# Weighted one-hot rows in a routing-weight build: split over VectorE, GpSimd and ScalarE

## The chip, the cores and the metric

The kernel runs on one core of one Trainium2 chip. The metric is device microseconds for one execution of the whole program. In the text PE is TensorE, DVE is VectorE, ACT is ScalarE, POOL is GpSimd and SP is SyncE, which here only issues DMAs.

## The reference, cut to what matters

The reference is one transformer layer over 512 tokens of width 2048: adaptive norm, a hybrid mixer (attention beside a gated recurrence), and then a PEER expert layer, which is where the change lies. For each token and each of 8 heads PEER picks 16 of 16,384 experts:

```python
v1, i1 = lax.top_k(s1, 16)            # 128 first keys
v2, i2 = lax.top_k(s2, 16)            # 128 second keys
vs, ic = lax.top_k(v1[..., :, None] + v2[..., None, :], 16)
e = i1[ic // 16] * 128 + i2[ic % 16]
w = jax.nn.softmax(vs, axis=-1)
...
act = jax.nn.gelu(jnp.einsum('thkd,td->thk', u[e], hx)) * wx
y   = jnp.einsum('thk,thkd->td', act, vt[e])
```

So a token has 128 picks (8 heads by 16), each with a first key, a second key and a weight. There are 16,384 experts, 128 by 128.

## The kernel before

Tokens 128 to 511 (three groups of 128) go through the experts densely. `ublock(b)` multiplies 128 experts' rows of u with the tokens: two half blocks, each a 512 KB load (`raw`), a rounded copy on ScalarE (`shi`, L91), the remainder on VectorE (`slo`, L92, `src - hi`) and 24 matmuls (L685). `shi` and `slo` have three buffers each, so the split can run at most a few half blocks ahead of TensorE. There are 128 such blocks. Their results are written to DRAM tables `tab1` and `tab2` (L691, L692).

Beside them the routing weights are built as a dense matrix, token by token, in six half sets of 64 tokens (the loop at L872; `hf` counts them). For each token a one-hot matrix of its 128 picks by first key (`o1`, four tokens in one VectorE operation, L880) is multiplied by a matrix of its picks by second key that carries the weight (`o2`, one operation per token, L885): row k of `o2` is the pick's weight at the column of its second key and zero elsewhere. TensorE multiplies the two (L886, two passes each for float32), four tokens share a PSUM bank, and ScalarE copies the bank into `ws` (L887). I call four tokens a group; there are 16 groups in a half set, 96 in all, 384 `o2` in all. `o2` has six buffers, so row matrices can be made a group and a half ahead of TensorE. After a half set `ws` is written to DRAM (L892) and VectorE takes its maximum in four operations (`F`, L893). After half sets 3 and 5 (counted from 0), `make_list` makes lists of the experts in use, scattered by GpSimd DMAs (L859).

Tokens 0 to 127 go another way, as side work: 128 gathers of rows of u (issued by GpSimd, L761, into four `gr` buffers), each followed by a dot product on VectorE (L775), then 128 gathers of rows of v, each followed by a multiply-add on VectorE (L773).

When all blocks are done, `vrun` gathers rows of v by the lists and multiplies them with the tables (L946), for two list sets in turn; what is left of the side work runs beside the first. The last part adds the residual and normalizes; its `xr` tiles hold pieces of the residual.

The order on each engine is not the source's: a scheduler places every instruction on its engine by a modelled timeline when the program is built. Each engine then works through its own queue strictly in that order and waits at its head.

Of the kernel before, what the change touches and what calls it, by code (L numbers as in the profile page):

```python
# [9 lines left out]
F32 = mybir.dt.float32  # L10
# [4 lines left out]
AF = mybir.ActivationFunctionType  # L15
OP = mybir.AluOpType
# [10 lines left out]
ND = 3  # L27
# [29 lines left out]
def program(ctx: ExitStack, tc: tile.TileContext, a):  # L57
    nc = tc.nc
    V, A, PE, G = nc.vector, nc.scalar, nc.tensor, nc.gpsimd

    def pool(stack, name, bufs=1, **kw):
        return stack.enter_context(tc.tile_pool(name=name, bufs=bufs, reuse_waits="tile", **kw))
# [20 lines left out]
    iota = const.tile([128, 128], F32, name="iota")  # L83
# [79 lines left out]
    def bank():  # L163
        return ps.tile([128, 512], F32, name="ps", tag="ps")

    def pbank():
        return ps.tile([128, 512], F32, name="pj", tag="pj", bufs=2)

    for q in range(4):
        p = pbank()  # L170
# [7 lines left out]
    with tc.tile_pool(name="pro", bufs=1, reuse_waits="tile") as pro:  # L178
# [7 lines left out]
        for t in range(NT):  # L186
# [10 lines left out]
            for k4 in range(4):  # L197
                p = pbank()
# [27 lines left out]
    def wt(dt=F32):  # L226
        return wk.tile([128, 512], dt, name="w" if dt == F32 else "wr", tag="w")
# [33 lines left out]
    p = pbank()  # L261
# [9 lines left out]
    p = bank()  # L271
# [31 lines left out]
    scale = 128 ** -0.5  # L303
# [213 lines left out]
    for q in range(4):  # L517
# [18 lines left out]
        for t in range(NT):  # L536
            for h in held:
                out_mm(t, *h)
            xr = wt()
# [17 lines left out]
    with tc.tile_pool(name="wk2", bufs=12, reuse_waits="tile") as wk2:  # L557
        for q in range(4):
            pr = bank()
            for k4 in range(4):  # L560
                k = q * 4 + k4
                p = bank()
# [78 lines left out]
    for h in range(H):  # L641
# [6 lines left out]
        for half in range(2):  # L648
            p = pbank()
# [10 lines left out]
            p = bank()  # L660
# [34 lines left out]
    otp = pool(dn, "otp", side="right")  # L695
    gq = pool(dn, "gq", 2, side="right")
    oT = []
# [7 lines left out]
    def ublocks(upto):  # L705
        while blk[0] < upto:
            ublock(blk[0])
            blk[0] += 1

    for t in range(ND):  # L710
        se, wv = decode(tp, tts[t])
        p = bank()
        o = otp.tile([128, 3, 128], F32, name="oT", bufs=ND)
        for i, src in enumerate((se[:, 0], se[:, 1], wv)):
            PE.transpose(p[:, i * 128:i * 128 + 128], src.rearrange("p h k -> p (h k)"), ident)
        A.copy(o, p[:, :384].rearrange("p (i t) -> p i t", i=3))
        oT.append(o)
        ublocks(t + 1)
    tk.close()
# [150 lines left out]
    with tc.tile_pool(name="dz", bufs=1, reuse_waits="tile") as dz:  # L870
        Fs = []
        sets = {}  # L872
        for hf, (t, h0) in enumerate(((1, 0), (1, 64), (2, 0), (2, 64), (0, 0), (0, 64))):
            ws = dz.tile([128, NB, TH], F32, name="ws")
            for t4 in range(TH // 4):
                ublocks(B0 + hf * BH + t4 * (BH - 3) // (TH // 4))
                p = bank()
                o1 = dz.tile([128, 4, 128], F32, name="o1", bufs=2)
                t0 = h0 + t4 * 4
                V.tensor_tensor(out=o1, in0=iota[:, None, :].to_broadcast([128, 4, 128]),  # L880
                                in1=oT[t][:, 0, t0:t0 + 4, None].to_broadcast([128, 4, 128]), op=OP.is_equal)
                for j in range(4):
                    tt = t0 + j
                    o2 = dz.tile([128, 128], F32, name="o2", bufs=6)
                    V.tensor_scalar(o2, iota, oT[t][:, 1, tt:tt + 1], oT[t][:, 2, tt:tt + 1], op0=OP.is_equal, op1=OP.mult)  # L885
                    PE.matmul(p[:, j * 128:j * 128 + 128], o2, o1[:, j], start=True, stop=True)  # L886
                A.copy(ws[:, :, t4 * 4:t4 * 4 + 4].rearrange("p i t -> p t i"), p.rearrange("p (t i) -> p t i", t=4))  # L887
            tab, c0 = (tab1, 128) if t == 0 else (tab2, 256 + (t - 1) * 128)
            F = dz.tile([128, NB], F32, name="F", bufs=4)
            for i in range(4):  # L890
                sl = slice(i * 32, i * 32 + 32)
                nc.sync.dma_start(tab[i * 4096:i * 4096 + 4096, c0 + h0:c0 + h0 + TH].rearrange("(i p) t -> p i t", p=128), ws[:, sl])  # L892
                V.tensor_reduce(F[:, sl], ws[:, sl], axis=AX.X, op=OP.max)  # L893
            Fs.append(F)
            if hf in (3, 5):
                m = Fs[0]
                for x in Fs[1:]:
                    V.tensor_tensor(out=m, in0=m, in1=x, op=OP.max)
                sets[hf // 4] = make_list(m, hf // 4)
                Fs = []  # L900
        ublocks(NB)
# [9 lines left out]
    fin = pool(vs_, "fin")  # L911
# [4 lines left out]
    for n in range(2):  # L916
        tot = sets[n][2]
        V.scalar_tensor_tensor(out=ov[:, n:n + 1], in0=tot[:, 1:2], scalar=float(-LISTS[n][2] * 128), in1=tot[:, 2:3],
                               op0=OP.add, op1=OP.max)
# [74 lines left out]
    nc.sync.dma_start(gf, bass.AP(tensor=a["g_final"].tensor, offset=a["g_final"].offset, ap=[[0, 128], [1, D]]))  # L994

    def pre_out(t, q, yq):
        xr = fin.tile([128, 512], F32, name="xr", bufs=4)
        nc.sync.dma_start(xr, xspill[t, q])
        V.tensor_tensor(out=yq, in0=yq, in1=ga2[q], op=OP.mult)  # L999
        V.tensor_tensor(out=yq, in0=yq, in1=xr, op=OP.add)  # L1000

    def square(t, q, yq):
        junk = fin.tile([128, 512], F32, name="junk")
        A.activation(junk, yq, AF.Square, accum_out=ssf[:, t, q:q + 1])
# [6 lines left out]
    def outs():  # L1011
        for t, yt in ((0, y0), (2, y[:, 0]), (3, y[:, 1])):
            for q in range(4):
                yq = yt[:, q * 512:q * 512 + 512]
                pre_out(t, q, yq)
                square(t, q, yq)
                yield
            r = inv(t)
            for half in range(2):
                hs_ = slice(half * 1024, half * 1024 + 1024)  # L1020
                V.scalar_tensor_tensor(out=yt[:, hs_], in0=yt[:, hs_], scalar=r, in1=gf[:, hs_], op0=OP.mult, op1=OP.mult)  # L1021
                nc.sync.dma_start(a["out"][0, t * 128:t * 128 + 128, hs_], yt[:, hs_])
                yield
        for q in range(4):
            pre_out(1, q, yo[:, q * 512:q * 512 + 512])
            yield
# [11 lines left out]
        pass  # L1038
    for q in range(4):
        qs = slice(q * 512, q * 512 + 512)  # L1040
        t_ = fin.tile([128, 512], F32, name="xr", bufs=4)
        V.tensor_tensor(out=t_, in0=banks[0][q], in1=ga2[q], op=OP.mult)  # L1042
        V.tensor_tensor(out=yo[:, qs], in0=t_, in1=yo[:, qs], op=OP.add)  # L1043
        square(1, q, yo[:, qs])
        V.tensor_tensor(out=yo[:, qs], in0=yo[:, qs], in1=gf[:, qs], op=OP.mult)  # L1045
# [63 lines left out]
```

## Time and profile before

| | us |
|---|---|
| median of 3 runs (3227.6 to 3237.68) | 3228.88 |
| the profiled execution | 3227.94 |
| its span, first to last instruction | 3226.1 |
| PE, DVE, ACT, POOL busy | 2978.0, 2507.4, 1225.5, 959.5 |

The span is one execution by the hardware profiler. An engine's busy time is a mean over stages with different limits. The first `o2` starts at 1247.8 us and the tables' last write from `ws` is issued just before 1810 us; I call what lies between the build stage. Before it, from 1075 us on, and after it, to 2342 us, the blocks run with the side work but without the build. TensorE's granted clock is 1.00 at 2.4 GHz and 0.50 at 1.2 GHz; a number between is a mean over a stretch.

### The profile page before, as it was taken

Reading aid. Unit: us, or ns where it says so; the run is one execution under the profiler, and the core shown is the slowest. Engines: PE = TensorE matmul, PEld = TensorE weight load, DVE = VectorE, ACT = ScalarE, POOL = GpSimd, SP = SyncE. Lnnn points to the kernel's source line nnn. Section 1 sums busy time; section 2 is a strip of 40 time slices with the busy share of each in tenths; the row PEclk is TensorE's granted clock in tenths of the full one; section 3 lists DMA queues with packets and bytes.
Section 4 is the critical chain, followed back from the end, with each engine's and each line's share of the span. In section 5 each row is a group of like instructions: output and inputs, shape, how many; then the busy total and the mean of one; then the engine's idle time right before and its main releaser. Section 6 shows DMA issues by size and latency. Waiting matters only on the chain. (4 is left out here: it accounts for less than half of the span.)

```text
span 3226.1 us, 40084 instructions
## 1 busy us (share of the span) xinstructions
PE 2978.0 (92%) x14597; PEld 2594.7 (80%) x14597; DVE 2507.4 (78%) x4073; ACT 1225.5 (38%) x1646; POOL 959.5 (30%) x668
## 2 busy tenths in 40 slices
PE   7899999989999999989899789999969999997787
PEld 6677778778788999989898789999957788886565
DVE  6877768762478899989999778888889855556787
ACT  5322224652322334334333222332233444444565
POOL 0000000000020002312225544444488644444774
PEclk9999899999999999989999899999989999998899
DMA  9777776243232457999998899999999976765996
GB/s 339 285 235 233 238 234 213 90 137 111 96 109 92 136 166 273 338 304 332 306 311 305 290 391 405 404 402 401 384 387 420 398 242 235 233 239 182 341 351 221
DMA packets 313124, 871.74 MB, mean 270 GB/s; under 512 B 125490, under 2 KB 164786, under 8 KB 258388
## 3 DMA queue, kind: packets, MB, share of 16 engines
q0 software_dynamic: 73376, 479.39, 39.0%
q1 hardware_dynamic: 239104, 389.52, 36.1%
q8 instruction: 116, 1.90, 0.2%
q14 instruction: 92, 0.75, 0.1%
q10 hardware_dynamic: 436, 0.18, 0.0%
HBM read 807.74 MB, written 61.25 MB: 269 GB/s over the span
## 5 line engine op out<-in xcount | busy, mean ns | idle before, releaser
L685 PE MATMUL pj<-dh,slo 128*128 128x384 f32 x2048 | 697.0, 341 | 39.4 <-DVE slo L92 38.9
L685 PE MATMUL pj<-dh,shi 128*128 128x384 f32 x2048 | 694.8, 339 | 12.2 <-ACT shi L91 12.2
L685 PE MATMUL pj<-dl,shi 128*128 128x384 f32 x2048 | 693.2, 338 | 0.0
L92 DVE TENSOR_TENSOR slo<-raw,shi 128x1024 fp32r<-128x1024 f32 (+1 forms) x402 | 485.4, 1215 | 237.3 <-ACT shi L91 235.8
L91 ACT CAST shi<-raw 128x1024 fp32r<-128x1024 f32 (+1 forms) x402 | 417.6, 1048 | 661.4 <-PE pj L685 256.1
L92 DVE TENSOR_TENSOR slo<-gr,shi 128x1024 fp32r<-128x1024 f32 x336 | 401.8, 1221 | 95.4 <-ACT shi L91 89.4
L685 PEld LDWEIGHTS pj<-dh,slo 128*128 128x128 f32 x2048 | 390.5, 191 | 45.3 <-DVE slo L92 44.9
L91 ACT CAST shi<-gr 128x1024 fp32r<-128x1024 f32 x336 | 342.0, 1046 | 204.3 <-PE ps L946 146.1
L685 PEld LDWEIGHTS pj<-dh,shi 128*128 128x128 f32 x2048 | 390.9, 191 | 13.9 <-ACT shi L91 13.7
L685 PEld LDWEIGHTS pj<-dl,shi 128*128 128x128 f32 x2048 | 390.2, 191 | 0.1
L946 PE MATMUL ps<-shi,gh 128*128 128x512 f32 x866 | 321.9, 412 | 69.3 <-ACT gh L91 55.2
L761 POOL DMA_INDIRECT gr<-u_rows,ei x128 | 200.5, 1567 | 526.1 <-DVE gr L775 295.4
L946 PE MATMUL ps<-slo,gh 128*128 128x512 f32 x866 | 350.8, 406 | 2.3 <-DVE slo L92 2.3
L946 PE MATMUL ps<-shi,gl 128*128 128x512 f32 x866 | 327.5, 402 | 13.2 <-DVE gl L92 13.2
L145 DVE SCALAR_TENSOR_TENSOR araw<-araw,sil 128x1024 f32<-128x1024 f32 x192 | 233.6, 1222 | 105.1 <-DMA araw<-w_ada 101.9
L773 DVE SCALAR_TENSOR_TENSOR y<-gr,dots,y 128x2048 f32<-128x2048 f32 x128 | 300.9, 2351 | 4.8 <-DMA gr<-v_rows,ei 2.7
L775 DVE SCALAR_TENSOR_TENSOR gr<-gr,hrow 128x2048 f32<-128x2048 f32 x128 | 290.7, 2282 | 14.0 <-DMA gr<-u_rows,ei 13.8
L761 POOL DMA_INDIRECT gr<-v_rows,ei x128 | 214.0, 1672 | 224.4 <-DVE y L773 189.7
L761 POOL DMA_INDIRECT raw<-tab,ig x159 | 246.0, 1547 | 112.6 <-DVE gl L92 82.5
L674 POOL CAST dh<-hh 128x384 fp32r<-128x384 f32 x16 | 10.4, 650 | 856.9 <-DVE hh L570 856.9
L946 PEld LDWEIGHTS ps<-shi,gh 128*128 128x128 f32 x866 | 168.2, 196 | 120.6 <-ACT gh L91 62.4
L761 POOL DMA_INDIRECT gr<-v_rows,iv x159 | 200.9, 1263 | 166.9 <-DVE slo L92 131.6
(345 smaller groups left out, 4955.8 us busy)
## 6 DMA issues: line engine op xcount, KB each, us to landing
raw<-peer_u SPq DMA_DIRECT2D x256, 512.0 KB, 8.1
araw<-w_ada SPq DMA_DIRECT2D x192, 512.0 KB, 5.2
raw<-w_in SPq DMA_DIRECT2D x66, 512.0 KB, 4.9
tab<-ws SPq DMA_DIRECT2D x24, 1024.0 KB, 13.0
raw<-w_out SPq DMA_DIRECT2D x32, 512.0 KB, 3.6
raw<-w_q SPq DMA_DIRECT2D x32, 512.0 KB, 3.6
tab<-ge SPq DMA_DIRECT2D x128, 128.0 KB, 5.2
tab<-ge SPq DMA_DIRECT2D x128, 64.0 KB, 6.4
```

Of the source, the lines that this page charges most:

```text
L91: A.copy(hi, src)
L92: V.tensor_tensor(out=lo, in0=src, in1=hi, op=OP.subtract)
L145: V.scalar_tensor_tensor(out=r, in0=r, scalar=1.0, in1=sil[:, half * 1024:half * 1024 + 1024], op0=OP.mult, op1=OP.mult, accum_out=acc[:, ...
L674: G.tensor_copy(dh[k], wh2[k][:, 128:])
L685: PE.matmul(p[:, :NDT], l[:, k8 * 128:k8 * 128 + 128], r, start=(k == 0 and i == 0), stop=(k == KC - 1 and i == 2))
L761: G.indirect_dma_start(out=out, out_offset=None, in_=src, in_offset=bass.IndirectOffsetOnAxis(ap=idx, axis=0))
L773: V.scalar_tensor_tensor(out=y0, in0=r, scalar=dots[:, j:j + 1], in1=y0, op0=OP.mult, op1=OP.add)
L775: V.scalar_tensor_tensor(out=r, in0=r, scalar=1.0, in1=hrow, op0=OP.mult, op1=OP.mult, accum_out=dots[:, j:j + 1])
L946: PE.matmul(banks[t][half * 2 + q2], l[:, ts], x[:, sl], start=first and i == 0, stop=last and i == 2)
```

## The change

Three things change. The tile `oT`, which holds the transposed first keys, second keys and weights, gets a fourth plane with the negated weights, made by one more ScalarE operation per token group. Of four `o2` in a group, the first is now made on ScalarE in two operations, |b - i| and then relu(w - w|b - i|), which is w where the column i is the second key b and 0 elsewhere since keys are whole numbers and w is positive; the second and the fourth are made on GpSimd and the third on VectorE, by the operation that all four had before. The `xr` tiles at the end of the kernel have three buffers for four.

```diff
-        o = otp.tile([128, 3, 128], F32, name="oT", bufs=ND)
+        o = otp.tile([128, 4, 128], F32, name="oT", bufs=ND)
...
-        A.copy(o, p[:, :384].rearrange("p (i t) -> p i t", i=3))
+        A.copy(o[:, :3], p[:, :384].rearrange("p (i t) -> p i t", i=3))
+        A.activation(o[:, 3], p[:, 256:384], AF.Copy, scale=-1.0)
...
-                    V.tensor_scalar(o2, iota, oT[t][:, 1, tt:tt + 1], oT[t][:, 2, tt:tt + 1], op0=OP.is_equal, op1=OP.mult)
+                    b_, w_, nw = (oT[t][:, i, tt:tt + 1] for i in (1, 2, 3))
+                    if j == 0:
+                        A.activation(o2, iota, AF.Abs, bias=b_, scale=-1.0)
+                        A.activation(o2, o2, AF.Relu, bias=w_, scale=nw)
+                    else:
+                        (G if j % 2 else V).tensor_scalar(o2, iota, b_, w_, op0=OP.is_equal, op1=OP.mult)
...
-        xr = fin.tile([128, 512], F32, name="xr", bufs=4)
+        xr = fin.tile([128, 512], F32, name="xr", bufs=3)
...
-        t_ = fin.tile([128, 512], F32, name="xr", bufs=4)
+        t_ = fin.tile([128, 512], F32, name="xr", bufs=3)
```

The scheduler lays out the queues anew. In the rows below a number at the end of a name only tells one buffer from another, `o_` rows with a width of 128 are `o2`, and those of width 512 are `o1`.

GpSimd's queue at the start of the build stage, before: after a small set-up (L730) come 81 gathers of the side work in a row, and then the scatters of the first list.

```order
L675 COPY dl<-hlo 128x384
L730 IOTA pm 128x1
L761 DMA gr<-u_rows,ei 128x2048 x81
L859 DMA list_88<-ig_15366,lidx_15389 2048x1 x15
L761 DMA gr<-u_rows,ei 128x2048
L859 DMA list_88<-ig_15366,lidx_15389 2048x1
```

The same place now (the gather is L762, the row matrix L891):

```order
L731 IOTA pm 128x1
L762 DMA gr<-u_rows,ei 128x2048
L891 TENSOR_SCALAR o_9505<-iota,oT 128x128
L891 TENSOR_SCALAR o_9511<-iota,oT 128x128
L891 TENSOR_SCALAR o_9522<-iota,oT 128x128
L762 DMA gr<-u_rows,ei 128x2048 x3
L891 TENSOR_SCALAR o_9528<-iota,oT 128x128
L891 TENSOR_SCALAR o_9608<-iota,oT 128x128
L891 TENSOR_SCALAR o_9614<-iota,oT 128x128
L762 DMA gr<-u_rows,ei 128x2048 x2
```

Gathers and row matrices alternate to the end of the build, 89 gathers and 192 row matrices; 65 of the gathers stand directly ahead of a row matrix.

VectorE's queue at the end of the third half set, before: between one `slo` and the next stand the four maxima, a dot product, one `o1` and five `o2`.

```order
L92 TENSOR_TENSOR slo<-raw,shi 128x1024
L893 TENSOR_REDUCE F<-ws 128x32 x4
L775 SCALAR_TENSOR_TENSOR gr,dots<-gr,hrow 128x2048
L885 TENSOR_SCALAR o_14102<-iota,oT 128x128
L885 TENSOR_SCALAR o_14105<-iota,oT 128x128
L885 TENSOR_SCALAR o_14183<-iota,oT 128x128
L880 TENSOR_TENSOR o_14181<-iota,oT 128x512
L885 TENSOR_SCALAR o_14186<-iota,oT 128x128
L885 TENSOR_SCALAR o_14189<-iota,oT 128x128
L92 TENSOR_TENSOR slo<-raw,shi 128x1024
```

The same place now (the maxima are L899, the dot product L776):

```order
L92 TENSOR_TENSOR slo<-raw,shi 128x1024
L899 TENSOR_REDUCE F<-ws 128x32 x4
L776 SCALAR_TENSOR_TENSOR gr,dots<-gr,hrow 128x2048
L881 TENSOR_TENSOR o_14234<-iota,oT 128x512
L891 TENSOR_SCALAR o_14243<-iota,oT 128x128
L92 TENSOR_TENSOR slo<-raw,shi 128x1024
```

Four `o2` have left this piece; the maxima still stand together ahead of the next `slo`.

ScalarE's queue in the midst of the build, before: `ws` copies between the rounded copies of the blocks.

```order
L91 CAST shi<-raw 128x1024
L887 COPY ws<-ps 128x4x128
L91 CAST shi<-raw 128x1024
L689 ACTIVATE ge<-pj 128x384
L91 CAST shi<-raw 128x1024
L887 COPY ws<-ps 128x4x128
```

The same now, in the second half set (`ws` copy is L893):

```order
L888 ACTIVATE o_11844<-iota,oT 128x128
L893 COPY ws<-ps 128x4x128
L91 CAST shi<-raw 128x1024
L889 ACTIVATE o_11844<-o_11844,oT 128x128
L888 ACTIVATE o_11932<-iota,oT 128x128
L893 COPY ws<-ps 128x4x128
L889 ACTIVATE o_11932<-o_11932,oT 128x128
L91 CAST shi<-raw 128x1024
```

The two operations of a row matrix stand around a `ws` copy, ahead of a `shi`. The queues hold no activation table load in the build stage, before or now.

## Rows read from the trace of the kernel before

**Rows 1.** Windows: us, busy PE, PEld, DVE, ACT, POOL (instructions), clock, DMA share, GB/s.

```profile
1200.00:1250.00 50.00, 50.00 (x291) 50.00 (x290) 49.53 (x132) 17.93 (x21) 1.41 (x2) 1.00 0.51 161
...
1247.80:1810.00 562.20, 511.16 (x3035) 500.12 (x3033) 539.32 (x891) 208.29 (x235) 171.06 (x112) 0.95 0.95 322
...
1600.00:1650.00 50.00, 37.09 (x197) 34.45 (x196) 48.93 (x112) 13.40 (x16) 7.13 (x5) 0.86 0.96 293
...
1910.00:2300.00 390.00, 389.89 (x2250) 389.57 (x2249) 327.07 (x206) 113.25 (x141) 166.98 (x94) 1.00 1.02 404
...
2350.00:2550.00 200.00, 170.21 (x696) 133.89 (x696) 177.83 (x161) 69.79 (x90) 166.00 (x107) 0.92 1.00 408
```

**Rows 2.** Groups by line, 1245 to 1800 us (busy us, mean ns, idle before).

```profile
L775 DVE SCALAR_TENSOR_TENSOR gr<-gr,hrow 128x2048 f32<-128x2048 f32 x92 | 209.6, 2280 | 2.5 <-DMA gr<-u_rows,ei 2.3
...
L885 DVE TENSOR_SCALAR o<-iota,oT 128x128 f32<-128x128 f32 x384 | 116.3, 345 | 16.0 <-PE ps L886 15.8
...
L92 DVE TENSOR_TENSOR slo<-raw,shi 128x1024 fp32r<-128x1024 f32 x93 | 112.8, 1214 | 0.5 <-ACT shi L91 0.5
...
L886 PE MATMUL ps<-o,o 128*128 128x128 f32 x768 | 114.7, 291 | 20.8 <-DVE o L880 10.4 <-ACT ws L887 6.7 <-DVE o L885 3.7
```

**Rows 3.** Waits, 1245 to 1800 us: who for whom, us, times, longest.

```profile
POOL gr L761 <- DVE gr L775: 232.3, 53, 18.3
...
PE pj L685 <- DVE slo L92: 22.9, 10, 7.8
...
PE ps L886 <- DVE o L880: 10.4, 19, 1.6
...
PE ps L886 <- ACT ws L887: 6.7, 1, 6.7
...
PE ps L886 <- DVE o L885: 3.7, 2, 3.4
```

**Rows 4.** Timelines of PE and DVE: start us, us, what [idle before it].

```profile
1407.57 1.50 PE L886 MATMUL ps<-o,o 128*128 128x128 f32 x12
...
1408.82 0.42 PE L685 MATMUL pj<-dh,slo 128*128 128x384 f32 x1
...
1435.57 0.69 PE L685 MATMUL pj<-dh,slo 128*128 128x384 f32 x1 [5.35 <-DVE slo L92]
...
1600.12 8.85 DVE L893 TENSOR_REDUCE F<-ws 128x32 f32<-128x2048 f32 x4
...
1612.37 0.69 PE L685 MATMUL pj<-dh,slo 128*128 128x384 f32 x1 [7.78 <-DVE slo L92]
```

**Rows 5.** Timelines of POOL and DVE where both worked, 879 to 897 us.

```profile
879.95 0.98 DVE L571 TENSOR_TENSOR hlo<-w,hh 128x512 fp32r<-128x512 f32 x1
...
883.77 0.69 DVE L571 TENSOR_TENSOR hlo<-w,hh 128x512 fp32r<-128x512 f32 x1
...
894.07 0.51 POOL L674 CAST dh<-hh 128x384 fp32r<-128x384 f32 x1
...
894.52 0.51 POOL L675 CAST dl<-hlo 128x384 fp32r<-128x384 f32 x1
...
895.90 1.57 DVE L92 TENSOR_TENSOR slo<-raw,shi 128x1024 fp32r<-128x1024 f32 x1 [5.30 <-ACT shi L91]
...
896.33 1.51 POOL L675 CAST dl<-hlo 128x384 fp32r<-128x384 f32 x1
```

**Rows 6.** ScalarE groups, whole span, that lie nearest to the new operations.

```profile
L441 ACT ACTIVATE w<-w,lp 128x512 f32<-128x512 f32 x8 | 6.5, 815 | 0.0
...
L442 ACT ACTIVATE w<-w 128x512 f32<-128x512 f32 x8 | 5.1, 634 | 0.0
...
L631 ACT ACTIVATE wv<-wv 128x128 f32<-128x128 f32 x4 | 1.2, 310 | 0.0
```

**Rows 7.** The side work's second half, and the gathers, from the page.

```profile
L773 DVE SCALAR_TENSOR_TENSOR y<-gr,dots,y 128x2048 f32<-128x2048 f32 x128 | 300.9, 2351 | 4.8 <-DMA gr<-v_rows,ei 2.7
...
L761 POOL DMA_INDIRECT gr<-u_rows,ei x128 | 200.5, 1567 | 526.1 <-DVE gr L775 295.4
```

## The prediction

> **What bounds the kernel now.** I read the busy times stage by stage first, because the change touches one stage. The reader is to see in [rows 1] that TensorE is full just before the build stage (50.00 of 50 us) and after it (389.89 of 390, granted clock 1.00), and that it is not full within it: from 1247.8 to 1810 us it is busy 511.2 of 562.2 us at a mean clock of 0.95. In the same stretch VectorE is busy 539.3 us, 96%, and the DMA engines 0.95. So in this stage alone VectorE is as near to a bound as TensorE.
>
> How much could the stage give? After it 2250 matmuls take 390 us, 0.1733 us each. The build stage holds 3035, of which 768 are the one-hot products [rows 1, 2]. The other 2267 need 392.8 us at that pace. Twelve one-hot products take 1.25 us to the start of what follows them [rows 4], 0.104 each, so 768 need 80.0. TensorE needs 472.8 us and the stage takes 562.2: 89.4 us are lost, 51.0 of them idle and 38.4 to matmuls that run slower, at a lower clock or spread out.
>
> Next the waits [rows 3]. Of the idle time, 22.9 us are waits for `slo`, 10.4 for `o1`, 6.7 for a `ws` copy and 3.7 for `o2`. Nearly all of it is VectorE being late. The timeline shows that the largest pieces have one form: 7.78 us at 1612.37 and 5.35 us at 1435.57 [rows 4], each after the maxima at the end of a half set, which hold VectorE for 8.85 us together. In the slice with the 7.78 us the granted clock is 0.86 [rows 1], so an idle piece costs clock as well.
>
> **The change part by part.** The sum is made against the profiled execution, 3227.94 us; the median of the runs is 0.9 us above it.
>
> *Row matrices leave VectorE.* 384 take 116.3 us [rows 2], 0.303 each; 288 go: 87.2 us less on VectorE.
>
> *192 of them come to GpSimd.* No row shows this operation on GpSimd. What matters first is what it takes from VectorE. Where both work, a subtraction of 128x512 on VectorE takes 0.98 instead of 0.69 us, and one of 128x1024 takes 1.57 where such ones take 1.21; GpSimd casts 384 columns at these moments [rows 2, 5]. So a GpSimd operation held VectorE 0.29 to 0.36 us, and GpSimd's next cast took 1.51 instead of 0.51. The new operation has a third of the columns, but compares, multiplies and reads two scalars. Low end: a third of 0.29, 0.10 us. High end: the casts' whole spacing, 0.45 us. I take two passes over a third of the columns, two thirds of 0.29 to 0.36, middle 0.22. That gives back 42 us of the 87 (19 to 86). VectorE is relieved by 45 us (1 to 68).
>
> The Trainium skill, "SBUF — State Buffer", section "SBUF: two separate sides", says that VectorE and GpSimd share a pair of ports under an exclusive lock, held for a whole instruction, with the loser blocked fully; the lengthened rows above agree with it. The Trainium skill, "GPSIMD Engine Reference", section 3.1, gives about 2.6 cycles an element at 1.2 GHz for elementwise work there, with which 128 columns are an estimated 0.28 us, and the same sum would come to 3216 instead of 3212.
>
> *What that is worth on TensorE.* Not all idle time can go. The 6.7 us for `ws` waits for DMA writes and stays. The 13.1 us after the maxima stay but for about 1 us each: in the new order the four maxima still stand together ahead of the next `slo`, with four `o2` fewer behind them. What can go is 22.9 - 13.1 + 2 for `slo`, 10.4 for `o1` and 3.7 for `o2`: 25.9 us. I let it go in the share in which VectorE is relieved, 45 of 87, 0.52: 13.4 us (0 to 20). Slower matmuls cost 0.75 us for each us idle (38.4 to 51.0); as the long stalls, which lower the clock most, remain, I count half of that: 5 us (0 to 15).
>
> *96 come to ScalarE, in two operations.* A 128x128 operation takes 0.310 us there, and two operands per partition add 0.815 - 0.634 = 0.18 [rows 6]. So Abs with one costs 0.40 and Relu with two 0.49 us: 96 times 0.89 is 85 us. ScalarE goes from 208 to 294 of 562 us [rows 1], which its own idle time hides. Behind such a pair waits a `shi`, behind that a `slo` and 24 matmuls. The `shi` comes 0.89 us later where a half block takes 24 times 0.1733 = 4.2, so I count 0; were the cover gone, 96 times 0.89 would be the price, 85 us.
>
> *Order elsewhere.* VectorE does 89 dot products to the end of the build before and 88 now, TensorE 2114 block matmuls there and now 2131; that is no term. Of the side work's second half, 88 gathers stand ahead of `vrun` where 90 did. So two more multiply-adds of 2.35 us [rows 7] fall into the stretch from 2350 to 2550 us, where VectorE is busy 177.8 of 200 us and TensorE loses 29.8 [rows 1]. That is 0 to 4.7 us later; I take 2.4.
>
> *The rest.* The fourth plane of `oT` is three more operations of about 0.4 us on ScalarE, ahead of the build, hidden by the blocks that it stands among. With three `xr` buffers the fourth load starts later; its steps come every second chunk of `vrun`, so I count 0, and not more than 2 us if the tail feels it.
>
> Sum: 3227.94 - 13.4 - 5 + 2.4 = 3212 us. The forecast's own range is 3200 to 3222.
>
> **The rivals.**
>
> *GpSimd's queue makes it slower.* GpSimd's gathers wait for VectorE to free a buffer: 53 times, 232.3 us in all [rows 3], 4.4 us each, and then take 1.57 us to issue [rows 7]. That cost nothing while nobody waited for GpSimd's queue. Now 65 of 89 gathers stand directly ahead of a row matrix that TensorE needs, and 4.4 + 1.57 = 6.0 us is about a group's time, 562 / 96 = 5.9. For it speaks this tie; against it, that six `o2` buffers let a row be made a group and a half ahead, and that the order was laid out so that gathers find their buffers. Place: TensorE waiting for `o2` made on GpSimd. If one in four of the 65, 16, is late by one dot product (2.28 us), TensorE idles 36 us more: 3212 + 36 = 3248. From 7 such rows on (16 us) the change is worth nothing, and beyond them it is slower.
>
> *The port takes it all back.* At the high end, 0.45 us held for each of 192, VectorE gains 1 us, and 2.4 us come on top: 3230, no change. For it speaks that the operation is compare, multiply and two scalars; against it, that the held time of the casts, 0.29 to 0.36, was less than their spacing.
>
> *More than forecast.* If VectorE gets ahead enough to absorb the maxima too, the DMA engines bind next: 0.95 of 562.2 us at the 1.02 that they sustain after the stage [rows 1] is 524 us, 38 us less: 3190. TensorE's 473 us would be lower still but is not reached for that reason. Against it: VectorE's maxima come right when `ws` is full, and lead is limited by three `slo` buffers, two half blocks or 8.4 us.
>
> **How the numbers follow.** A difference under 0.3%, 9.7 us, can hardly be told from none here. Forecast 0.43; port 0.18; GpSimd's queue 0.24; more than forecast 0.15. The forecast's range reaches 4 us into the band of no change, so I move 0.04 of it there. Faster by over 0.3% (below 3218): 0.39 + 0.15 = 0.54. Within: 0.18 + 0.04 = 0.22. Slower: 0.24. The time is the forecast's, 3212. For 8 in 10 I go from 3178, which holds most of the larger gain, to 3250, which holds the GpSimd rival at its price.
>
> **What would show it.** Right: in the build stage VectorE's busy time falls by about 45 us and its subtractions, with GpSimd beside them, are longer on average than 1.21 us; TensorE waits less for `slo` and `o1`, and 5 to 8 us still at each end of a half set; the stage is some 18 us shorter. The held time is wrong if `slo` and the dot products lengthen by clearly more or less than 42 us together. The rival on GpSimd's queue shows as TensorE's products waiting for row matrices of GpSimd by over 20 us, with gathers ahead of them waiting for VectorE. ScalarE's cover was not there if `slo` waits for `shi` in the stage, where it hardly did (0.5 us, [rows 2]). What would make the whole wrong is a build stage that is as long as before while VectorE is no longer full.

## The result, and the profile after

The changed kernel takes 3364.44 us (median of 4 runs, 3363.01 to 3368.76) against 3228.93 before: ratio 1.0416, 95% interval 1.0395 to 1.0437. The forecast was 3212, with a range from 3178 to 3250.

I split each span at two events: the build, from the first one-hot product to the last, the blocks from there to the last block's product, and the rest. Ahead of the build both kernels take 1252 to 1253 us.

| kernel | build | blocks | rest | span |
|---|---|---|---|---|
| before | 526.8 | 563.2 | 883.9 | 3226.1 |
| after | 601.2 | 622.5 | 884.6 | 3361.2 |

So 74 us are lost in the stage that the change touches, 59 in a stage of which it touches no line, and nothing behind it. The stages are those of one execution each; two kernels that hold the same number of products in each (the kernel before, and the one with B0 13 below) lie 7 us apart in the build and 4 in the blocks, so a difference of a few us says nothing. Windows of the kernel after, with the columns of [rows 1]: the build, and 340 us of the block stage.

```profile
1253.00:1854.00 601.00, 510.26 (x2902) 493.83 (x2901) 447.57 (x544) 263.63 (x416) 453.44 (x296) 0.92 0.85 284
...
1960.00:2300.00 340.00, 318.06 (x1718) 311.66 (x1717) 245.95 (x170) 87.81 (x109) 125.67 (x72) 0.95 0.95 354
```

The same two stretches of the kernel before:

```profile
1252.00:1779.00 527.00, 483.24 (x2890) 472.60 (x2888) 505.96 (x826) 201.29 (x228) 159.37 (x106) 0.95 0.94 322
1960.00:2300.00 340.00, 339.89 (x1961) 339.57 (x1960) 286.20 (x170) 98.24 (x123) 144.87 (x82) 1.00 1.02 403
```

In the build TensorE does as many matmuls as before (2902 and 2890), but is idle 91 us instead of 44, and its busy time is 27 us longer at a granted clock of 0.92 instead of 0.95: 47 + 27 = 74. VectorE, 96% busy before, is busy 447.57 of 601 us. In the block stage TensorE was full at a clock of 1.00; now it is idle 22 of 340 us at 0.95 and does 1718 matmuls where it did 1961.

What answers to [rows 2, 3 and 6], groups of the kernel after, 1245 to 1860 us:

```profile
L891 POOL TENSOR_SCALAR o<-iota,oT 128x128 f32<-128x128 f32 x192 | 305.7, 1597 | 81.1 <-PE ps L892 79.1
...
L776 DVE SCALAR_TENSOR_TENSOR gr<-gr,hrow 128x2048 f32<-128x2048 f32 x88 | 201.7, 2294 | 6.1 <-DMA gr<-u_rows,ei 6.1
L92 DVE TENSOR_TENSOR slo<-raw,shi 128x1024 fp32r<-128x1024 f32 x91 | 112.8, 1242 | 37.5 <-ACT shi L91 37.3
...
L891 DVE TENSOR_SCALAR o<-iota,oT 128x128 f32<-128x128 f32 x96 | 34.5, 359 | 28.2 <-PE ps L892 28.1
...
L889 ACT ACTIVATE o<-o,oT 128x128 f32<-128x128 f32 x96 | 46.9, 491 | 1.1
L888 ACT ACTIVATE o<-iota,oT 128x128 f32<-128x128 f32 x96 | 38.6, 402 | 157.3 <-PE ps L892 157.2
```

VectorE makes a row matrix in 0.36 us, GpSimd in 1.60 on average. VectorE's dot products and subtractions are hardly longer than in [rows 2] (2294 against 2280 ns, 1242 against 1214). The waits of TensorE in the kernel after, 1253 to 1854 us (who for whom: us, times, longest), show where the row matrices are missed:

```profile
PE ps L892 <- POOL o L891: 49.5, 38, 10.3
PE pj L685 <- DVE slo L92: 12.0, 8, 5.6
PE ps L892 <- ACT o L889: 11.4, 6, 4.1
PE pj L685 <- ACT shi L91: 7.5, 5, 3.5
PE ps L892 <- DVE o L881: 6.6, 2, 3.4
PE ps L892 <- ACT ws L893: 3.2, 2, 2.3
```

Before, from 1252 to 1779 us, the waits for `o1`, `ws` and `o2` are those of [rows 3]; the other two are:

```profile
PE pj L685 <- DVE slo L92: 19.3, 9, 7.8
...
PE pj L685 <- ACT shi L91: 3.2, 4, 1.2
```

Summed by the engine that TensorE waits for (the profile puts a wait down to what came last), VectorE falls from 33.4 to 18.6 us, ScalarE rises from 9.9 to 22.1, and GpSimd goes from nothing to 49.5. These three make up the 47 us. VectorE's `slo` also waits for `shi` now, 37.3 us (the L92 group above) where it waited 0.5 [rows 2].

Why a GpSimd row takes so long is seen in two timelines of the kernel after (start us, us, what), GpSimd first, then VectorE beside it:

```profile
1399.20 5.12 POOL L891 TENSOR_SCALAR o<-iota,oT 128x128 f32<-128x128 f32 x1
```

```profile
1399.33 2.28 DVE L776 SCALAR_TENSOR_TENSOR gr<-gr,hrow 128x2048 f32<-128x2048 f32 x1
...
1401.54 2.28 DVE L776 SCALAR_TENSOR_TENSOR gr<-gr,hrow 128x2048 f32<-128x2048 f32 x1
```

One row of 128 columns spans two whole dot products, and these keep the length that they have without it. The longest of the 38 waits is of another kind. TensorE, and then GpSimd at the end of that wait:

```profile
1681.00 1.22 PE L892 MATMUL ps<-o,o 128*128 128x128 f32 x4 [10.32 <-POOL o L891]
```

```profile
1677.80 0.97 POOL L860 DMA_INDIRECT list<-ig,lidx  x1 [0.30 <-issue]
1679.08 1.00 POOL L762 DMA_INDIRECT gr<-u_rows,ei  x1 [0.30 <-issue]
1680.13 2.36 POOL L891 TENSOR_SCALAR o<-iota,oT 128x128 f32<-128x128 f32 x3
```

Here the row stands behind a run of scatters of the first list in GpSimd's own queue. Laid over GpSimd's timeline, the 49.5 us are 37.9 in which it is at a row, 6.3 at these scatters and 3.1 at the issue of a gather, with the rest between issues; in none of them does a gather wait for its buffer.

In the block stage the waits are new too (kernel after, 1960 to 2300 us; before, TensorE was idle 0.1 us there):

```profile
PE pj L685 <- ACT shi L91: 15.5, 10, 1.6
PE pj L685 <- DVE slo L92: 6.4, 10, 0.7
```

ScalarE and then TensorE around one of these ten, in the kernel after:

```profile
2114.77 0.49 ACT L689 ACTIVATE ge<-pj 128x384 f32<-128x384 f32 x1 [7.83 <-PE pj L685]
2115.16 2.93 ACT L91 CAST shi<-raw 128x1024 fp32r<-128x1024 f32 x3
```

```profile
2114.22 0.33 PE L685 MATMUL pj<-dl,shi 128*128 128x384 f32 x1
2114.40 0.34 PE L685 MATMUL pj<-dh,slo 128*128 128x384 f32 x1
2116.25 0.44 PE L685 MATMUL pj<-dh,shi 128*128 128x384 f32 x1 [1.51 <-ACT shi L91]
...
2117.51 0.69 PE L685 MATMUL pj<-dh,slo 128*128 128x384 f32 x1 [0.65 <-DVE slo L92]
2117.99 0.52 PE L685 MATMUL pj<-dh,shi 128*128 128x384 f32 x1
2118.31 0.52 PE L685 MATMUL pj<-dl,shi 128*128 128x384 f32 x1
```

ScalarE sits 7.83 us in front of a gelu (`ge`) that can't begin until TensorE ends the block. The copies (`shi`) of the next block stand behind it in ScalarE's queue, so TensorE has nothing when the block ends: 1.51 us for the copy, 0.65 for its rest, and then matmuls 0.32 us apart instead of 0.17. From 2118 to 2120 us the granted clock is 0.50, the lower of its two levels.

ScalarE's queue in the block stage, before (x counts equal ones in a row):

```
L91 CAST shi<-raw 128x1024 x4
L689 ACTIVATE ge<-pj 128x384 x2
L91 CAST shi<-raw 128x1024 x3
L689 ACTIVATE ge<-pj 128x384
L91 CAST shi<-raw 128x1024
L689 ACTIVATE ge<-pj 128x384
```

And after:

```
L91 CAST shi<-raw 128x1024 x4
L689 ACTIVATE ge<-pj 128x384
L91 CAST shi<-raw 128x1024
L689 ACTIVATE ge<-pj 128x384
L91 CAST shi<-raw 128x1024 x3
L689 ACTIVATE ge<-pj 128x384 x2
```

The same items in another phase. A block has two copies. I call *lead* the copies that stand ahead of a gelu beyond those of its own block and the blocks before it. Over the gelus behind the last `ws` copy, the lead before is 1, 2 or 3 and only at the two ends 0; after, it is 2 or 1 and in 16 of 63 cases 0.

### The profile page after: what moved, and what is told of

The parts are those of the page before. It is cut to its first block, busy times and chain, and to the rows that moved or that the text cites. A ratio compares the mean times of both kernels' runs of the same rounds, so it can differ in the third digit from the quotient of the medians.

```text
span 3361.2 us, 40293 instructions
## 1 busy us (share of the span) xinstructions
PE 3024.5 (90%) x14597; PEld 2626.4 (78%) x14597; DVE 2443.3 (73%) x3785; ACT 1288.7 (38%) x1841; POOL 1242.0 (37%) x860
## 5 line engine op out<-in xcount | busy, mean ns | idle before, releaser
L685 PE MATMUL pj<-dh,slo 128*128 128x384 f32 x2048 | 715.3, 350 | 53.3 <-DVE slo L92 53.3
L685 PE MATMUL pj<-dh,shi 128*128 128x384 f32 x2048 | 711.0, 347 | 30.8 <-ACT shi L91 30.7
L92 DVE TENSOR_TENSOR slo<-raw,shi 128x1024 fp32r<-128x1024 f32 (+1 forms) x402 | 487.5, 1223 | 333.6 <-ACT shi L91 328.5
L685 PE MATMUL pj<-dl,shi 128*128 128x384 f32 x2048 | 706.4, 345 | 0.0
L92 DVE TENSOR_TENSOR slo<-gr,shi 128x1024 fp32r<-128x1024 f32 x336 | 402.1, 1222 | 99.3 <-ACT shi L91 94.0
L685 PEld LDWEIGHTS pj<-dh,slo 128*128 128x128 f32 x2048 | 402.6, 197 | 61.9 <-DVE slo L92 61.9
L685 PEld LDWEIGHTS pj<-dh,shi 128*128 128x128 f32 x2048 | 402.5, 197 | 36.9 <-ACT shi L91 36.8
L685 PEld LDWEIGHTS pj<-dl,shi 128*128 128x128 f32 x2048 | 401.3, 196 | 0.1
L891 POOL TENSOR_SCALAR o<-iota,oT 128x128 f32<-128x128 f32 x192 | 305.7, 1597 | 81.1 <-PE ps L892 79.1
L674 POOL CAST dh<-hh 128x384 fp32r<-128x384 f32 x16 | 10.3, 645 | 856.1 <-DVE hh L570 856.1
L762 POOL DMA_INDIRECT gr<-v_rows,ei x128 | 219.2, 1712 | 275.3 <-DVE y L774 235.5
L776 DVE SCALAR_TENSOR_TENSOR gr<-gr,hrow 128x2048 f32<-128x2048 f32 x128 | 292.1, 2292 | 28.4 <-DMA gr<-u_rows,ei 28.4
L762 POOL DMA_INDIRECT gr<-u_rows,ei x128 | 185.7, 1451 | 242.8 <-DVE gr L776 136.2
L762 POOL DMA_INDIRECT raw<-tab,ig x159 | 231.0, 1453 | 117.2 <-DVE gl L92 86.2
L762 POOL DMA_INDIRECT gr<-v_rows,iv x159 | 200.8, 1263 | 171.3 <-DVE slo L92 135.7
```

The costliest lines, as they stand in the source:

```text
L92: V.tensor_tensor(out=lo, in0=src, in1=hi, op=OP.subtract)
L674: G.tensor_copy(dh[k], wh2[k][:, 128:])
L685: PE.matmul(p[:, :NDT], l[:, k8 * 128:k8 * 128 + 128], r, start=(k == 0 and i == 0), stop=(k == KC - 1 and i == 2))
L762: G.indirect_dma_start(out=out, out_offset=None, in_=src, in_offset=bass.IndirectOffsetOnAxis(ap=idx, axis=0))
L776: V.scalar_tensor_tensor(out=r, in0=r, scalar=1.0, in1=hrow, op0=OP.mult, op1=OP.mult, accum_out=dots[:, j:j + 1])
L891: (G if j % 2 else V).tensor_scalar(o2, iota, b_, w_, op0=OP.is_equal, op1=OP.mult)
```

## The experiments

Each was run beside the kernel before on the same chip, and the ratios are to that: 3234.11 us beside the first four, 3234.91 beside the next four and 3236.16 beside the last four. The first four were made before the lead had been counted; their theory for the block stage was the order of the loads and writes on SP's queue.

**ScalarE's part alone.** VectorE makes the other three rows.

```
-  (G if j % 2 else V).tensor_scalar(o2, iota, b_, w_, ...)
+  V.tensor_scalar(o2, iota, b_, w_, ...)
```

> Only the first of four row matrices moves, to ScalarE; the other three stay on VectorE, none on GpSimd. In the changed kernel the last one-hot product came 75 us later (1854 for 1779 us) and the block stage behind it took 59 us more (622 for 563). Theory T: these are two causes. The first 75 us are GpSimd's row matrices. The 59 us are the queue order that the scheduler gives the block stage, two table writes and then four loads on SP (and two gelu results ahead of the rounded copies on ScalarE), where before writes and loads alternate. This kernel has no GpSimd rows but that same later order, so T expects a build that ends at 1765 to 1780 us, a block stage of about 620 and a total near 3280. Rival R1, all 135 us come from GpSimd's rows, the later stage too: block stage 563, total 3210 to 3230. Rival R2, ScalarE's two operations delay the build: last product past 1800 us.

3307.02 us, ratio 1.0214 (1.0194 to 1.0233): build 523.8, blocks 641.3. The theory had the build right; the blocks came 21 us above its 620 and the time 27 above its 3280. The block stage is hurt without any GpSimd row. The build's 3 us less are no gain, as 57 block products fewer fall into it. TensorE waits 21.3 us for VectorE in it (33.4 before) and 27.8 for ScalarE (9.9 before), 10.7 of these for the new rows: what a row of four off VectorE (some 29 us) gives, ScalarE takes.

**GpSimd's part alone.**

```
-  if j == 0:
+  if j in ():
```

> Only the second and fourth row matrix move, to GpSimd; the others stay on VectorE, ScalarE makes none. The block stage has the alternating order of the kernel before. Theory T: build 50 to 75 us longer (last product at 1830 to 1855 us), block stage about 563, total 3280 to 3305. R1 (GpSimd's rows throw the later stage out of step too): block stage about 620, total near 3350. R2 (ScalarE's rows are the cost): build near 1779 us, total near 3230.

3349.98, ratio 1.0353 (1.0320 to 1.0386): build 588.6, blocks 615.2. The build is 62 us longer with GpSimd's rows alone, so most of the 74 is theirs. The blocks were expected at 563 and came where the rival R1 had them. SP's queue alternates here as in the kernel before (three loads, a block's writes, one load, a block's writes), and the block stage is lost all the same.

**The changed kernel with other block counts, and the kernel before with others,** meant to make SP's queue alternate as it did before, or stand in pairs as it does after:

```
-BH = 18        (changed kernel)      -B0 = 12        (kernel before)
+BH = 19                              +B0 = 13
```

> The changed kernel with one number different: 19 instead of 18 blocks are due per half set (BH), which gives the block stage the alternating order of writes and loads that the kernel before has. All row matrices stand as in the change. Theory T: build as long as in the changed kernel (last product near 1850 us), block stage near 563 instead of 622 us, total 3300 to 3310. R1: block stage near 620, total near 3364.

> The kernel before with one number different: 13 instead of 12 blocks come ahead of the build (B0), which gives the block stage the order of the changed kernel, two writes and then four loads. All row matrices on VectorE. Theory T: build within 10 us of 1779, block stage near 620 us, total 3280 to 3290. R1: block stage near 563, total near 3228.

3359.09 (1.0379, 1.0357 to 1.0401) with blocks 622.3, and 3232.09 (0.9986, 0.9970 to 1.0002) with blocks 566.9. The theory missed both, but neither edit did what it was meant to. In the traces SP's queue of the first still has two blocks' writes and then four loads, all through the block stage, and that of the second still three loads and one load in turn (SP of the first, then of the second, around 2110 us; x is how many in a row):

```profile
2113.11 8.10 SPq L96 DMA_DIRECT2D raw<-peer_u  x4
```

```profile
2107.37 3.94 SPq L96 DMA_DIRECT2D raw<-peer_u  x3
...
2115.16 0.38 SPq L96 DMA_DIRECT2D raw<-peer_u  x1
```

So these two do not test the SP order. It falls by others: GpSimd's part alone loses the block stage with the alternating order, and three runs below (the changed kernel, and one and two ScalarE rows, with the lead kept) do not lose it with pairs. Both kept the lead of the kernel that they came from, which led to the next two.

**The lead, given back and taken away.** In the changed kernel, the gelu gets its scale from a one-element operation that reads the next block's first copy:

```
+  one = gq.tile([128, 1], F32, name="one")
+  A.activation(one, uh[:, :1], AF.Identity, scale=0.0, bias=ones[:, :1])
-  A.activation(ge, p[:, :NDT], AF.Gelu_apprx_tanh)
+  A.activation(ge, p[:, :NDT], AF.Gelu_apprx_tanh, scale=one)
```

> The changed kernel, but in the u blocks from 60 on each gelu is queued on ScalarE behind the first rounded copy of the next block (a one-element operation that reads that copy hands the gelu its scale of 1.0), so that ScalarE is always at least one copy ahead when it waits for a block to end. Stages: build = first to last one-hot product, blocks = from there to the last block's product, rest. Theory (in the changed kernel 16 of 63 gelus of the block stage stand ahead of every copy of the next block, and TensorE then waits for that copy): build stays 598 to 604, blocks fall from 622 to 560 to 572, TensorE in 1960:2300 goes from 318 back to 335 to 340 of 340; time 3300 to 3318. Rival (the order of the gelus is only a symptom; the block stage is lost through the DMA order or through what stands ahead on VectorE): blocks stay 610 to 625, time 3355 to 3370.

In the kernel before, every fourth block's copy is made to wait for the last gelu:

```
+  if half == 0 and b >= 64 and b % 4 == 0:
+      A.activation(r[:, :1], last[0][:, :1], AF.Identity, scale=0.0, bias=r[:, :1])
```

> The kernel before, but from block 64 on every fourth block's first rounded copy is made to wait for the gelu of the block before it (a one-element operation that adds 0 times the gelu to the raw tile), so that 16 gelus of the block stage stand ahead of every copy of the next block, as in the changed kernel. One-hot rows all on VectorE, no GpSimd row. Theory: build stays 525 to 530, blocks rise from 563 to 595 to 625, time 3260 to 3292, the waits of the products are for the rounded copy and for the rest slo. Rival (the gelus' place costs nothing by itself): blocks 563 to 572, time 3228 to 3238.

3304.70 us (1.0216, 1.0186 to 1.0247) with build 600.9 and blocks 558.6; and 3305.07 with build 519.9 and blocks 632.8, ratio 1.0239 (1.0198 to 1.0281). Windows of the first, then of the second:

```profile
1960.00:2300.00 340.00, 340.00 (x1963) 340.00 (x1962) 278.35 (x189) 116.37 (x164) 153.79 (x83) 1.00 1.01 400
```

```profile
1960.00:2300.00 340.00, 318.20 (x1734) 310.71 (x1734) 251.11 (x157) 93.21 (x120) 125.31 (x72) 0.95 0.95 360
```

TensorE is full at full clock in the changed kernel, GpSimd rows and all, and stalls in the kernel before to the same 318 us. The gelus' place is the cause of the block stage's loss. The first came out 1 us below its block range. The second is 5 us below its build range and 8 above its block range, since some 50 block products (8.7 us) moved from the one stage to the other; its time is 13 us above. Behind the blocks the two take 8 and 10 us more than the kernel before, for which no cause was sought.

The runs with the whole side work in one table. "0 leads" counts the gelus behind the last `ws` copy that have none. TensorE is its busy time in 1960:2300 with the granted clock. As the order moves some blocks between the stages, the last column has the block stage per block product in it (2903 to 3071 of them), in ns.

| run | 0 leads | TensorE | blocks | ns each |
|---|---|---|---|---|
| before | 2 | 339.89, 1.00 | 563.2 | 186 |
| after | 16 | 318.06, 0.95 | 622.5 | 208 |
| ScalarE's part alone | 21 | 318.08, 0.95 | 641.3 | 209 |
| GpSimd's part alone | 17 | 318.09, 0.95 | 615.2 | 204 |
| changed, BH 19 | 16 | 318.07, 0.95 | 622.3 | 208 |
| before, B0 13 | 2 | 338.03, 0.99 | 566.9 | 188 |
| changed, lead kept | 1 | 340.00, 1.00 | 558.6 | 186 |
| before, lead taken | 17 | 318.20, 0.95 | 632.8 | 206 |
| ScalarE's part, lead kept | 1 | 340.00, 1.00 | 571.7 | 186 |
| two ScalarE rows, lead kept | 1 | 340.00, 1.00 | 543.4 | 187 |
| one row each on ScalarE and GpSimd | 3 | 339.88, 1.00 | 557.9 | 188 |

**What makes GpSimd's rows late.** The side work's dot products and multiply-adds on 64 of 2048 columns (the other columns are left out), in the changed kernel and in the kernel before; the gathers stay. Each was run once:

```
-  in0=r, scalar=1.0, in1=hrow
+  in0=r[:, :64], scalar=1.0, in1=hrow[:, :64]
```

> The changed kernel with the dot products and multiply-adds of the side work on 64 of their 2048 columns (the other columns are left out); the gathers stay whole. Looked at in the build alone. Theory (a GpSimd row of 0.78 us stands until VectorE's row of two-input operations is through): the mean of the 192 GpSimd rows falls from 1.60 to 0.9 to 1.2 us, their longest from 5.9 to under 3.5, and the build comes to within 25 us of the next run's. Rival (the GpSimd rows are late behind gathers in their own queue, and by their own length): their mean stays 1.4 or more, and the build stays 50 us or more above the next run's.

> The kernel before with the same 64 columns in the side work: the pair of the run ahead of it, which shows what shorter side work is worth without GpSimd rows. If VectorE's load bounds the build (about 100 dot products of 2.3 us fall in it): build 526.8 falls to 440 to 480. If it is bound by TensorE and by how products, sets and copies hang together (the run with a row of four on ScalarE took some 29 us off VectorE and its build fell by 3): build 500 to 525.

GpSimd's rows in the first, all of the run (ns: least, median, greatest); in the kernel after they are 780, 1050 and 5946:

```profile
L891 POOL TENSOR_SCALAR o<-iota,oT x192: 783/866/2439, 1249.4 to 1755.0; 128x128 f32<-128x128 f32 x192
```

Their mean falls from 1.60 to 1.12 us. Builds are 505.9 and 452.7, 53 us apart, which is outside what the theory gave and inside what the rival gave. But the two do not hold the same work: the order moved blocks, 2711 matmuls against 2503, and TensorE is busy 456.79 and 415.20 us, 42 of the 53. Its idle time is 49 of 506 us (9.7%) with GpSimd rows and 37 of 452 (8.2%) without, where with the whole side work it is 91 of 601 (15.1%) and 44 of 527 (8.3%). So 12 of 47 us of extra idle time are left. Products wait 19.4 us for GpSimd's rows instead of 49.5, and 8.9 of these are one wait behind list scatters. The kernel before's shorter build lies in the range that was given for a build bound by VectorE's load. But it too holds less work, 2503 matmuls instead of 2890, which is 68 of its 74 us, at the same idle share, so it does not show that this load bounded the build. The gathers waited for buffers as before (1250 to 1760 us; the kernel after, then this run):

```profile
POOL gr L762 <- DVE gr L776: 39.1, 12, 7.8
```

```profile
POOL gr L762 <- DVE gr L776: 36.4, 18, 8.6
```

That clears the waiting gathers as the main cause and puts most of the extra idle time on VectorE's long operations. How much of it comes by way of the gathers' issue, which also fell, from 1.41 to 1.09 us each, these runs do not tell. Their lead had changed sides as well, by itself: blocks 579.7 in the changed one with a lead kept (one 0), 694.4 in the other with 19 of 71 at 0 (318.09 us, clock 0.95), and with its work cut that kernel is slower for it, 3273.27 us.

**ScalarE's part with its lead kept; two rows of four there; half the GpSimd rows.**

```
   if j in (0,):    A.activation(...) twice
   if j in (0, 2):  A.activation(...) twice
   if j in (0,):    A.activation(...) twice, and j == 1 on GpSimd
```

> One row of four on ScalarE, three on VectorE, none on GpSimd, and the gelus of blocks 60 on kept behind the first copy of the next block (as in the run of the changed kernel with its lead kept). Theory (block stage lost to the gelus' place alone, build lost to the GpSimd rows alone): build 518 to 530, blocks 555 to 566, time 3218 to 3240, the same as before within 0.3%. Rival (the ScalarE rows cost the block stage something of their own): blocks 580 or more, 3250 or more.

> Rows 0 and 2 of four on ScalarE (two operations each), 1 and 3 on VectorE, none on GpSimd, lead kept. It takes some 58 us off VectorE in the build and puts 170 on ScalarE. Theory (off VectorE is worth little: one row of four less gave 3 us of build; ScalarE has room, busy 261 of 524): build 512 to 532, blocks 555 to 566, time 3210 to 3240. Rival (copies of the u blocks come late behind two-operation rows on ScalarE): build 535 to 555, time 3245 to 3270.

> Row 0 of four on ScalarE, row 1 on GpSimd, 2 and 3 on VectorE: half the GpSimd rows of the changed kernel. By itself it keeps one copy of lead in the block stage (32 gelus with 1, 16 with 2, 12 with 3, 3 at the ends with 0), with no forced order. Theory (each GpSimd row that must wait for VectorE costs TensorE): TensorE's idle time in the build 60 to 75 (before 44, changed 91), build 545 to 575, blocks 558 to 570, time 3250 to 3285. Rival (GpSimd is late only when it has two rows of each four beside its gathers): build 522 to 535, time 3225 to 3240.

The first: ratio 0.9998 (0.9982 to 1.0014), build 520.2, blocks 571.7 (6 above its range, with 50 block products more in them than before): no change, as expected. The second: 1.0058 (1.0042 to 1.0074), build 561.7, blocks 543.4. Its build was expected at 512 to 532 and the time came to the rival's 3245 to 3270. Some of its build is only shifted (118 block products fewer stand behind it); together with the blocks it is 15 us longer than before. TensorE's waits in that build bear the rival out: 30.2 us for ScalarE (`ws` copies 12.5, `shi` 10.8, rows 6.9) where they were 9.9 before, and 25.5 for VectorE where they were 33.4. The third: 1.0059 (1.0036 to 1.0081), build 560.1, blocks 557.9, TensorE idle 65.5 of 550 us: in the theory's range, but for the blocks, 0.1 us under it. Half the GpSimd rows cost about half the extra idle time (22 of 47 us; without any it is 4, in the first of these three), though here TensorE's waits are named for `ws` copies (17.6 us) and `shi` (13.4) more than for GpSimd's rows (5.9): a late row holds its bank, and the copy of the bank holds ScalarE's queue. That last link is read from the queue's order and was not tried by itself.

**The price of a GpSimd row by itself.** The kernel before with a tail (shortened here, and run once):

```
+  for k in range(8): G.tensor_scalar(z[k], z2[:, 0:128], s1, s2, op0=OP.is_equal, op1=OP.mult)
+  for k in range(10): V.tensor_tensor(out=z2[:, 1024:2048], in0=z2[:, 0:1024], in1=yo[:, 0:1024], op=OP.subtract)
```

and so beside dot products of 2048 columns, beside one-input maxima, and alone.

> The kernel before with a tail that measures GpSimd rows by themselves and beside VectorE: four rows of 128 columns alone, four copies of 128 columns, four rows of 512 columns; eight rows beside ten subtractions of 128x1024; eight beside eight dot products of 128x2048; eight beside eight one-input maxima; and four, each behind a gather, with VectorE at rest. Theory: a row alone 0.78 to 0.85 us; beside two-input operations the rows end only as VectorE's run ends (the first one 5 us or more, the mean of eight over 1.5), while VectorE's operations lengthen by under 0.15 us each; beside one-input maxima and behind gathers 0.78 to 0.95. Rival (they share turn by turn): rows 1 to 2 us each beside subtractions and dot products, and VectorE's operations 0.5 us or more longer while a row runs.

GpSimd's timeline of this tail (x is how many in a row; the rows stand alone, then a copy, then beside subtractions, dot products and maxima, and behind a gather):

```profile
3224.42 3.23 POOL L1059 TENSOR_SCALAR y<-yo,cols 128x128 f32<-128x128 f32 x4 [21.17 <-issue]
3227.62 0.99 POOL L1065 COPY y<-yo 128x128 f32<-128x128 f32 x4
...
3238.66 11.57 POOL L1059 TENSOR_SCALAR y<-y,cols 128x128 f32<-128x128 f32 x8 [1.36 <-DVE y L1069]
3254.80 20.11 POOL L1059 TENSOR_SCALAR y<-y,cols 128x128 f32<-128x128 f32 x8 [4.57 <-DVE y L1075]
3277.39 6.23 POOL L1059 TENSOR_SCALAR y<-y,cols 128x128 f32<-128x128 f32 x8 [2.49 <-DVE y L1082]
3298.44 0.81 POOL L1097 TENSOR_SCALAR y<-y,cols 128x128 f32<-128x128 f32 x1
```

VectorE beside the second and third of these:

```profile
3237.34 1.23 DVE L1069 TENSOR_TENSOR y<-y,yo 128x1024 f32<-128x1024 f32 x1 [12.70 <-POOL y L1059]
3238.60 13.62 DVE L1073 TENSOR_TENSOR y<-y,yo 128x1024 f32<-128x1024 f32 x10
...
3257.07 2.42 DVE L1079 SCALAR_TENSOR_TENSOR y<-y,yo 128x2048 f32<-128x2048 f32 x1
```

A row is 0.81 us alone and behind a gather, 0.78 beside maxima, 1.45 beside subtractions (11.57 / 8) and 2.51 beside dot products (20.11 / 8): about one row per VectorE operation. My theory had said that rows end only when VectorE's whole run ends; that fell here. That VectorE hardly pays held: 1.36 for a subtraction (13.62 / 10) instead of 1.23. In the kernel a row did stand through two dot products (5.12 us); the tail's longest was 2.89. What makes that difference is open. The two timelines differ in one thing at least: in the tail a dot product starts 0.12 us after the last one begins to hand over its sum (3259.41 and 3259.53 us), in the kernel at the same moment (1401.54).

## Why the prediction was wrong, step by step

- **The first sentence failed: "the change touches one stage".** 59 us come from the block stage, which it gave no term. Two lines on order stand in the prediction ("that is no term"; behind a pair on ScalarE "waits a `shi`", counted 0), and both look at the build alone. The changed queue of the block stage could be read beforehand: the zero leads are in ScalarE's order. That TensorE was full there at clock 1.00 [rows 1] should have sent me to look: such a stage has nothing to give and all to lose.
- **GpSimd's rows: the direction was wrong.** "What matters first is what it takes from VectorE" was put at 42 us (0.22 each). Measured, the dot products and subtractions lengthened by 14 and 28 ns, 3.8 us over 88 and 91 of them. What counted was what VectorE takes from GpSimd: rows of 0.81 us alone became 1.60, and TensorE waited 49.5 us for them, 10.3 of it behind list scatters in GpSimd's queue. The rows that I had for it, [rows 5], already held this: the cast of 0.51 us that took 1.51 beside a subtraction. I read that as the upper end of VectorE's price and not as GpSimd's. The Trainium skill, "SBUF — State Buffer", section "SBUF: two separate sides", has the lock held for a whole instruction, with the loser blocked fully. The trace agrees for GpSimd, of which one row passes per VectorE operation in the tail. It does not for VectorE: ten subtractions took 1.3 us longer beside eight rows of 0.81. The estimate of 0.28 us from "GPSIMD Engine Reference", section 3.1, of the Trainium skill fits the copy here (0.99 / 4 = 0.25) but not the row, 0.81.
- **What relief of VectorE is worth on TensorE: near, and taken back elsewhere.** I let 13.4 us idle go for 45 us of relief. VectorE was busy 58 us less (505.96 to 447.57) and TensorE's waits for it fell by 14.8. That did not shorten the build, since the waits for the engines that took the rows rose by 61.7; so the 5 us of clock did not come either (0.92 instead of 0.95). In ScalarE's part alone the two sides also cancel, and with its lead kept the whole time did not change (0.9998). The reading "Nearly all of it is VectorE being late" was too strong: the waits for VectorE in [rows 3] are 37.0 of the 51.0 us.
- **ScalarE: the price was right, "hides" was not.** The operations take 0.40 and 0.49 us, 85.5 us together, as worked out. But products wait 11.4 us for these rows, and for ScalarE in all 12.2 us more than before, where I counted 0: I had asked only whether the `shi` behind a pair comes in time, and not whether the row does. The sign that I named for it came: `slo` waits 37.3 us for `shi` (8.1 with ScalarE's rows alone and the lead kept). And its place in ScalarE's queue changes the lead: by itself it brings 21 zero leads.
- **"The rest", and the two multiply-adds:** 0.7 us more behind the blocks (2.4 forecast), too little to tell from none.
- **The rival that was slower** had the place (products waiting for GpSimd's rows, over 20 us) and the sign, at half the price, 36 us where the build lost 74. Its mechanism, gathers that wait for a buffer ahead of a row, is not the main one: in none of the 38 waits does GpSimd stand waiting for a gather's buffer, and the gathers wait as long in the short side work, while TensorE's extra idle time falls from 47 to 12 us. A gather's earlier wait may still make a later row late; no run separates that.
- **The sign that I named for "the whole wrong"** came: the build is not shorter while VectorE is no longer full.

What remains open: why ScalarE's rows, or two GpSimd rows, move the gelus by a phase while one of each does not; the order is settled before the run, and I did not trace its rule.

No version that does all the work beat the kernel before. The nearest, one row on ScalarE with the lead kept, is the same within its interval.

## What to carry to other kernels

When a change adds instructions to a queue that runs far ahead, compare the order of that queue in the later stages too, and count how many of the next unit's inputs stand ahead of each operation that waits for the bound engine: where none does, the bound engine stalls, and the clock falls with it. Before work goes to GpSimd beside a VectorE that is busy with two-input operations, price it by the VectorE operation that it must wait out, and ask who waits for the result. A busy share of 96% does not say what relief is worth: sum the bound engine's waits by the engine that it waits for, before and after, since what one engine gives back the engines that take its work can use up.

## What the hardware showed that I had not expected

- A compare-and-multiply of 128x128 with two per-partition scalars takes GpSimd 0.81 us, a copy of the same size 0.25.
- Beside two-input VectorE operations about one such row passes per VectorE operation, 1.45 or 2.51 us each, while these lengthen by about 0.1 us (a subtraction from 1.23 to 1.36); beside one-input maxima there is no effect (0.78).
- Stalls of 2.2 us every 34 us (10 in 340) lower TensorE's mean granted clock to 0.95 and cost 12% of its matmuls, where its idle time is 6.5%.
